# Moving six of sixteen row tiles of p @ w_ple away from attention, into the router's gap and in front of the tail

## The chip, the cores and the metric

The kernel runs on one core of one Trainium2 chip. A core has five engines that run side by side and wait for each other by semaphores: PE (TensorE, matrix products into the banks of PSUM), DVE (VectorE), ACT (ScalarE), POOL (GpSimd) and SP (SyncE, which here issues most DMAs). Each engine works through its own row of instructions in order. The metric is the time of one execution on the device, in microseconds (us).

## The reference

One encoder layer over x (2048 rows of 1024, f32). What follows is the order of the work, cut to what matters here:

```python
h = rms_norm(x, g_mix);  q, k, v, u = split(h @ w_in)
ya = attention_group(q, k, v)        # 8 query heads, 2 key heads of 64, all 2048 keys
yh = hyena_group(u)                  # two gated long convolutions by FFT, 512 channels
x = x + concat(group_rms(ya), group_rms(yh)) @ w_out
x = x + hierarchical_moe(rms_norm(x, g_moe))      # 32 experts, two per row
gate = sigmoid(rms_norm(x, g_ple) @ w_ple_gate + b_ple_gate)
x = x + (p @ w_ple) * gate           # p: 2048 x 256, w_ple: 256 x 1024
return rms_norm(x, g_final)
```

The change is about `p @ w_ple`. It depends on nothing but inputs, so it can be computed at any time before the last gate; sixteen tiles of 128 rows make up the 2048 rows.

## The kernel before, in words

`block_kernel` writes the work of two sides in turn. The left side is the input projection and then `Attention.run`; the right side is the filters of hyena, hyena itself, and what follows it. `interleave` (L91) always takes the next piece from the side that has come less far, by costs that the pieces yield, scaled with `SHARE`. An engine runs its instructions in the order in which they come out of this, so the order is fixed when the program is built.

Attention works in units of one head and half of the queries (16 units). A unit has 16 steps over key tiles: score products L798 and L801 into a PSUM bank, exp on ACT (L802), and the products with v (L811). Between them stand the products L733 and maxima L735 that prepare later units. At a unit's end L833 sums the rows, SP carries the sums through DRAM, and L850 on DVE scales the output. Scores use two banks (pool `at_ps`); a third comes from the pool `at_px`, which is opened some units after the right side has said `K.banks_free = True`:

```python
wait -= K.banks_free
if wait == -BANKS_AFTER:
    psx = self.pool("at_px", 1, space=PSUM)
```

The pool is opened `BANKS_AFTER` = 2 units after the flag. Its bank lies where banks of the right side lay, and so the first product that uses it waits for the last user of these.

Hyena has three kinds of steps here. A pair is a transform back of one tile (L539 on PE, its gate L541 on DVE, named z) followed by the next transform (L499). A middle step (`mid`) loads zt and ab, multiplies by w (L294, tile ph<-zt), multiplies by the filter on DVE (L523, tile ab), goes back (L307, tile ph<-ab), and is copied by ACT (L527) and stored. The last transforms back are L539 and L541 alone. All of them share one PSUM tile of two banks, ph.

p @ w_ple is computed in two ways. `Ple` splits p and w_ple into a high and a low fp32r part: per tile two transposes L1514, and for each of two column halves six products L1529 to L1531, a copy to the SBUF tile ob by ACT (L1532; two buffers), and when both halves are there a store to DRAM, pp_d, by SP (L1534). `LatePle` uses plain f32, L1570, and keeps its result in SBUF. Before the change tiles 0 to 3 are late (`PLE_LATE`), 4 to 6 run on the right side behind hyena (`PLE_N`), after a delay that counts as progress (`PLE_LAG`), and 7 to 15 run behind `stage_out`, while the router works out which row goes to which expert: that stretch is called the router's gap. The router's small products there are L1131, L1157, L1158, L1169 and L1170; its tile ep holds the number of blocks of each expert. SP reads these numbers one by one into registers (L1359, 31 TENSOR_LOADs), and also issues the store and the load of a small table (L1221, tile ov_eb; L1223, tile ebr).

The experts start with casts of the raw weights on ACT (L1301), products L1322 to L1324 and, for rows beyond full blocks, f32 products L1328. The tail loads rows x and the experts' results, normalises them (xn, DVE L1635), transposes them (L1642), multiplies by w_ple_gate (L1652 to L1654) and combines the gate with the product pp. Its tile t takes pp from SBUF where it is late, else it loads it from pp_d (`Tail.tiles`, L1611). `LatePle.run` stands just ahead of it in PE's row.

## Time and profile before

| | us |
|---|---|
| median of three runs | 3171.41 (3170.64 to 3173.77) |
| the profiled execution | 3178.87 |
| its span | 3177.1 |
| PE busy | 2905.4 (91%) |
| DVE busy | 2047.3 (64%) |
| ACT busy | 1322.0 (42%) |
| POOL busy | 1143.2 (36%) |

The profiled execution is one of its own, 7.46 us longer than the median of the runs, and 1.8 us of it lie outside the span. In the timeline's rows an idle time in brackets stands behind an instruction that its engine had to wait for, with what released it last. Products on PE overlap, so one that is shown with 0.40 us may start 0.23 us behind the one ahead of it. PEclk in the windows is the granted clock as a share of 2.4 GHz.

### The profile page before, as it was taken

The numbers are of one execution on the slowest core, as the hardware profiler recorded it, in microseconds if no ns is written. First come the engines' busy times: TensorE is split into PE (matmuls) and PEld (weight loads), VectorE is DVE, ScalarE is ACT, GpSimd is POOL, SyncE is SP. The second block draws the span as 40 slices with busy tenths as digits, with TensorE's granted clock in tenths as the row PEclk, the third lists the DMA queues.
The fourth block names the chain that finished last, engine by engine and source line by source line (L and its number), as shares of the span: only waits on it lengthen the run. The fifth ranks groups of instructions, "written<-read, shape, count | busy, mean of one in ns | idle before, by whom it ended". The sixth has DMA issues, their size and how long they took to land. (4 is left out here: it accounts for less than half of the span.)

```text
span 3177.1 us, 50424 instructions
## 1 busy us (share of the span) xinstructions
PE 2905.4 (91%) x19001; PEld 1937.3 (61%) x19001; DVE 2047.3 (64%) x2737; ACT 1322.0 (42%) x1975; POOL 1143.2 (36%) x1058
## 2 busy tenths in 40 slices
PE   7989889798899999759999999989999999998897
PEld 5757667575445453524444488856667777675776
DVE  5865656536677776628887745366667677675665
ACT  3232233332344434225444422245556566664332
POOL 1423323242355555218877643011111211121443
PEclk9989889898999999879999999989999999999999
DMA  6477787786755765651000254379789888897553
GB/s 196 146 219 245 212 251 238 225 262 187 222 164 171 204 179 168 177 170 44 18 12 15 65 168 140 137 230 337 249 274 340 292 305 284 309 322 250 180 180 112
DMA packets 471989, 627.45 MB, mean 197 GB/s; under 512 B 64597, under 2 KB 302984, under 8 KB 467262
## 3 DMA queue, kind: packets, MB, share of 16 engines
q1 hardware_dynamic: 451630, 568.73, 55.7%
q0 software_dynamic: 20112, 55.47, 5.5%
q8 instruction: 150, 2.46, 0.3%
q14 instruction: 97, 0.79, 0.1%
HBM read 462.45 MB, written 161.56 MB: 196 GB/s over the span
## 5 line engine op out<-in xcount | busy, mean ns | idle before, releaser
L1306 DVE TENSOR_TENSOR wl<-raw,wh 128x1024 fp32r<-128x1024 f32 x384 | 462.8, 1223 | 202.2 <-ACT wh L1301 192.8
L1301 ACT CAST wh<-raw 128x1024 fp32r<-128x1024 f32 x384 | 398.2, 1051 | 262.9 <-PE ps L1324 87.5
L821 POOL TENSOR_TENSOR sums<-e,sums 128x512 f32<-128x512 f32 x306 | 412.4, 1364 | 145.9 <-ACT e L802 135.7
L802 ACT ACTIVATE e<-ps 128x512 f32<-128x512 f32 x512 | 290.1, 596 | 330.8 <-PE ps L801 278.5
L735 DVE TENSOR_REDUCE mx<-pa 128x1 f32<-128x512 f32 x512 | 330.1, 683 | 100.9 <-PE pa L733 100.2
L811 PE MATMUL po<-e,v 128*64 128x512 f32 x1024 | 290.0, 624 | 0.0
L1401 POOL DMA_DIRECT2D y_d<-ob x64 | 36.0, 564 | 556.8 <-DVE ob L1400 349.4
L1322 PE MATMUL ps<-wh,xt 128*128 128x512 f32 (+4 forms) x512 | 212.8, 416 | 9.5 <-ACT wh L1301 9.3
L1323 PE MATMUL ps<-wl,xt 128*128 128x512 f32 (+4 forms) x512 | 207.5, 405 | 7.1 <-DVE wl L1306 7.1
L1324 PE MATMUL ps<-wh,xt 128*128 128x512 f32 (+4 forms) x512 | 203.6, 398 | 0.0
L148 PE MATMUL ps<-xh,wh 128*128 128x512 f32 x384 | 157.7, 411 | 8.1 <-ACT U L204 8.1
L733 PE MATMUL pa<-kst,q 128*128 128x512 f32 x352 | 140.3, 450 | 22.6 <-DVE mx L735 20.2
L149 PE MATMUL ps<-xl,wh 128*128 128x512 f32 x384 | 159.3, 415 | 0.0
L150 PE MATMUL ps<-xh,wl 128*128 128x512 f32 x384 | 158.0, 411 | 0.4 <-POOL wl L88 0.4
L88 POOL TENSOR_TENSOR wl<-raw,wh 128x2048 fp32r<-128x2048 f32 (+1 forms) x26 | 102.8, 3956 | 150.3 <-ACT wh L138 144.8
L798 PE MATMUL ps<-q,kst 128*128 128x512 f32 x352 | 151.5, 431 | 3.6 <-ACT e L802 3.6
L801 PE MATMUL ps<-q,k 65*128 65x512 f32 x352 | 141.9, 403 | 4.7 <-DMA q<-mr 4.7
L821 DVE TENSOR_TENSOR sums<-e,sums 128x512 f32<-128x512 f32 x110 | 120.5, 1102 | 34.7 <-ACT e L802 34.0
L733 PEld LDWEIGHTS pa<-kst,q 128*128 128x128 f32 x352 | 63.3, 191 | 123.1 <-DVE mx L735 73.0
L1271 POOL DMA_INDIRECT g<-h_d,idx x52 | 74.5, 1433 | 165.5 <-PE pt L1289 66.4
L148 PE MATMUL ps<-wh,xh 128*128 128x256 f32 x384 | 121.6, 317 | 4.7 <-ACT xh L79 2.4
L1322 PEld LDWEIGHTS ps<-wh,xt 128*128 128x128 f32 (+4 forms) x512 | 96.0, 188 | 47.0 <-ACT wh L1301 13.7
(370 smaller groups left out, 6631.5 us busy)
## 6 DMA issues: line engine op xcount, KB each, us to landing
raw<-in_w_gate_dram SPq DMA_DIRECT2D x128, 512.0 KB
raw<-in_w_up_dram SPq DMA_DIRECT2D x128, 512.0 KB
raw<-in_w_down_dram SPq DMA_DIRECT2D x128, 512.0 KB
h_f<-hs SPq DMA_DIRECT2D x256, 128.0 KB
ab<-h_f SPq DMA_DIRECT2D x32, 1024.0 KB
raw<-in_w_in_dram SPq DMA_DIRECT2D x30, 1024.0 KB
xt<-in_x_dram SPq DMA_DIRECT2D x32, 512.0 KB
dec<-in_c_decay_dram SPq DMA_DIRECT2D x64, 256.0 KB
```

Of the source, the lines that this page charges most:

```text
L148: nc.tensor.matmul(ps, lh, rh, start=(k == 0), stop=False)
L149: nc.tensor.matmul(ps, lh, rl, start=False, stop=False)
L733: nc.tensor.matmul(pa, qh[:, t * P:(t + 1) * P], self.kst[g][:, q * 512:(q + 1) * 512], start=True, stop=True)
L735: nc.vector.tensor_reduce(out=mx[:, t, q:q + 1], in_=pa, axis=AX.X, op=ALU.max)
L802: nc.scalar.activation(out=pe[:, i], in_=ps, func=AF.Exp, scale=0.125)
L811: mm = nc.tensor.matmul(po[H2[i]], v[:, kt, g * 64:(g + 1) * 64], pe[:, i], start=(kt == 0), stop=(kt == NT - 1), skip_group_check=True)
L821: acc[j][1].tensor_tensor(out=sums[j], in0=pe[:, i], in1=src, op=ALU.add)
L1301: nc.scalar.copy(hi, raw)
L1306: nc.vector.tensor_tensor(out=lo, in0=raw, in1=hi.bitcast(F32), op=ALU.subtract)
L1322: nc.tensor.matmul(ps[:m], xt[:, k, 0, :m], hv[:, j], start=(k == 0), stop=False)
L1323: nc.tensor.matmul(ps[:m], xt[:, k, 0, :m], lv[:, j], start=False, stop=False)
L1324: nc.tensor.matmul(ps[:m], xt[:, k, 1, :m], hv[:, j], start=False, stop=(k == 7))
```

## The change

The three tiles of the right side are taken away, together with their delay, their own loading of the weights and their numbers (`PLE_N`, `PLE_LAG`, the fourth share). The router's gap takes tiles 6 to 15, ten instead of nine, and tiles 0 to 5 are late, six instead of four. `LatePle` transposes its rows in two groups of four and two tiles, the pool for pp in the tail has six buffers instead of four, and `Tail.tiles` loads x for the tiles 4 and 5 itself, without a load of pp.

```diff
@@ -42,11 +42,9 @@
 SUM_POOL = [2] * 16
 PV_LAG = 2
 BANKS_AFTER = 2
-PLE_N = 3
 ROUTE_AT = 0
-PLE_LATE = 4
-PLE_LAG = 5.0
-SHARE = (0.56, 1.0, 0.8, 1.6)
+PLE_LATE = 6
+SHARE = (0.56, 1.0, 0.8)
 
 
 def rows_bcast(ap, parts=P):
@@ -1551,10 +1549,12 @@
             pr = px.tile([P, PLE_LATE, 256], F32, name="pr")
             nc.sync.dma_start(pr, p_in[:PLE_LATE * P].rearrange("(t p) n -> p t n", p=P))
             for k in range(2):
-                pt = pst.tile([P, 512], F32, tag="pt", name="pt")
-                for t in range(PLE_LATE):
-                    nc.tensor.transpose(pt[:, t * P:(t + 1) * P], pr[:, t, k * P:(k + 1) * P], K.ident)
-                nc.scalar.copy(self.pT[:, k].rearrange("p t c -> p (t c)"), pt[:, :PLE_LATE * P])
+                for t0 in range(0, PLE_LATE, 4):
+                    pt = pst.tile([P, 512], F32, tag="pt", name="pt")
+                    n = min(4, PLE_LATE - t0)
+                    for t in range(n):
+                        nc.tensor.transpose(pt[:, t * P:(t + 1) * P], pr[:, t0 + t, k * P:(k + 1) * P], K.ident)
+                    nc.scalar.copy(self.pT[:, k, t0:t0 + n].rearrange("p t c -> p (t c)"), pt[:, :n * P])
 
     def run(self, pool):
 
@@ -1582,7 +1582,7 @@
         self.K, self.x1_d, self.pp_d = K, x1_d, pp_d
         pool = lambda name, bufs, **k: st.enter_context(tc.tile_pool(name=name, bufs=bufs, **k))
         pc, self.pl, praw = [pool(f"ta_{n}", b, side=K.side) for n, b in (("c", 1), ("l", 4), ("raw", 2))]
-        pw, self.pp = pool("ta_w", 2, side=K.side), pool("ta_p", 4)
+        pw, self.pp = pool("ta_w", 2, side=K.side), pool("ta_p", PLE_LATE)
         self.bc = {}
 
         with tc.issue_after(after):
@@ -1604,9 +1604,9 @@
         return x2
 
     def tiles(self, t):
-        if t < len(self.done):
-            return self.loaded.pop(0), self.done[t]
-        x2 = self.load(t)
+        x2 = self.loaded.pop(0) if self.loaded else self.load(t)
+        if t < PLE_LATE:
+            return x2, self.done[t]
         pp = self.pp.tile([P, D], F32, tag="pp", name="pp")
         self.K.nc.sync.dma_start(pp, self.pp_d[t * P:(t + 1) * P])
         return x2, pp
@@ -1826,12 +1826,6 @@
                     yield c * SHARE[2]
             s_hc.close()
             yield None
-            yield PLE_LAG * SHARE[3]
-            with ExitStack() as s1:
-                ple.open(s1, K.side)
-                ple.weights()
-                for c in ple.run(s1, range(PLE_LATE, PLE_LATE + PLE_N)):
-                    yield c * SHARE[3]
             K.banks_free = True
             pw = s_w.enter_context(tc.tile_pool(name="ou_w", bufs=2, side=K.side))
             with tc.tile_pool(name="ou_r", bufs=2, side=K.side) as praw:
@@ -1848,7 +1842,7 @@
                           A["b_group"], A["w_router"][0], A["b_router"], x1_d, h_d, lg, R, ple.weights)
             s_w.close()
             with ExitStack() as s2:
-                for n, _ in enumerate(ple.run(s2, range(PLE_LATE + PLE_N, NT), 3, K.side)):
+                for n, _ in enumerate(ple.run(s2, range(PLE_LATE, NT), 3, K.side)):
                     if n == ROUTE_AT:
                         R.finish(A["c_caps"])
             late = LatePle(K, st, A["p"][0, 0], A["w_ple"][0])
```

Line numbers of the kernel after are two lower than those before, up to the `Ple` class; L1570 and what follows it have the same numbers in both.

On PE, at the unit end that lies at 1236.28 us in the trace (sums are row sums, kst and k keys, bt and z tiles of hyena), the kernel before goes on like this:

```order
L833 MATMUL pa<-sums,sel 32x512 x3
L733 MATMUL pa<-kst_6073,qh 128x512 x2
L539 MATMUL ph<-bt,wb 64x512 x2
L798 MATMUL ps<-q_11301,kst_6073 128x512
L801 MATMUL ps<-q_11301,k_6074 128x512
L798 MATMUL ps<-q_11301,kst_6073 128x512
L801 MATMUL ps<-q_11301,k_6074 128x512
L833 MATMUL pa<-osq,sel 32x512
L733 MATMUL pa<-kst_6073,qh 128x512 x2
L499 MATMUL ph<-z,w1d 128x512 x2
L798 MATMUL ps<-q_11301,kst_6073 128x512
L801 MATMUL ps<-q_11301,k_6074 128x512
```

The kernel after, at the same unit end and then at the end of hyena's work:

```order
L831 MATMUL pa<-sums,sel 32x512 x3
L731 MATMUL pa<-kst_6073,qh 128x512 x2
L537 MATMUL ph<-bt,wb 64x512 x2
L831 MATMUL pa<-osq,sel 32x512
L731 MATMUL pa<-kst_6073,qh 128x512 x3
L497 MATMUL ph<-z,w1d 128x512 x2
L731 MATMUL pa<-kst_6073,qh 128x512 x4
L537 MATMUL ph<-bt,wb 64x512 x2
...
L305 MATMUL ph<-ab,wa 64x128 x32
L537 MATMUL ph<-bt,wb 64x512 x16
L796 MATMUL ps<-q_11344,kst_6073 128x512
L799 MATMUL ps<-q_11344,k_6074 128x512
```

Before, score products (L798, L801) stand between hyena's pairs; after, the first of them (L796, L799) stands behind the last of hyena's L537, with four pairs and eight middle steps ahead of it.

On PE in the router's gap (rt_ tiles are the router's, pr and ph, plh, pll are PLE's), before:

```order
L1131 MATMUL rt_ps<-rt_i_15551,rt_oh_15544 32x193
L1157 MATMUL rt_ps<-rt_f_17623,rt_i_15554 128x32
L1158 MATMUL rt_ps<-rt_f_17623,rt_i_15554 64x32
L1514 MATMUL pt<-ident,pr 128x128 x2
L1529 MATMUL pp<-plh,ph 128x512
L1530 MATMUL pp<-pll,ph 128x512
L1531 MATMUL pp<-plh,pl 128x512
L1529 MATMUL pp<-plh,ph 128x512
L1530 MATMUL pp<-pll,ph 128x512
L1531 MATMUL pp<-plh,pl 128x512
L1169 MATMUL rt_ps<-ident,rt_f_17638 128x32 x2
```

And after:

```order
L1129 MATMUL rt_ps<-rt_i_15448,rt_oh_15441 32x193
L1512 MATMUL pt<-ident,pr 128x128 x2
L1527 MATMUL pp<-plh,ph 128x512
L1528 MATMUL pp<-pll,ph 128x512
...
L1529 MATMUL pp<-plh,pl 128x512
L1155 MATMUL rt_ps<-rt_f_17520,rt_i_15451 128x32
L1156 MATMUL rt_ps<-rt_f_17520,rt_i_15451 64x32
L1527 MATMUL pp<-plh,ph 128x512
...
L1529 MATMUL pp<-plh,pl 128x512
L1167 MATMUL rt_ps<-ident,rt_f_17535 128x32 x2
```

The transposes of a tile and one column half have moved ahead of the router's first small products, and another half stands ahead of the next ones.

On SP, behind the register loads of ep and around the load of the table ebr, before:

```order
L1534 DMA pp_d<-ob 128x1024
L1223 DMA ebr<-ov_eb 1x128
L1359 TENSOR_LOAD ep
L1359 ISA x2
L1534 DMA pp_d<-ob 128x1024
L1359 TENSOR_LOAD ep
```

And after:

```order
L1532 DMA pp_d<-ob 128x1024
L1221 DMA ebr<-ov_eb 1x128
L1357 TENSOR_LOAD ep
L1357 ISA x2
L1357 TENSOR_LOAD ep
L1357 ISA x2
L1532 DMA pp_d<-ob 128x1024
L1357 TENSOR_LOAD ep
L1357 ISA x2
L1357 TENSOR_LOAD ep
L1357 ISA x2
...
L1357 ISA x2
L1532 DMA pp_d<-ob 128x1024
```

Before, the last store of pp_d stood one register load behind ebr. After, two stores stand behind it, the second behind six register loads.

## Rows read from the trace of the kernel before

**Rows 1.** Windows: stretch and length, busy us and (instructions) of each engine, granted clock, DMA share, GB/s.
```profile
core 0: us, PE busy (x) PEld busy (x) DVE busy (x) ACT busy (x) POOL busy (x), PEclk, DMA share, GB/s
1302.00:1390.00 88.00, 48.94 (x594) 29.21 (x593) 29.82 (x43) 6.66 (x7) 1.64 (x1) 0.65 0.63 177
1508.00:1736.00 228.00, 226.01 (x884) 105.85 (x887) 182.06 (x265) 103.74 (x188) 177.99 (x133) 1.00 0.07 17
2140.00:2400.00 260.00, 260.00 (x1382) 177.09 (x1380) 175.59 (x179) 150.91 (x183) 37.97 (x50) 1.00 0.82 288
```

**Rows 2.** Timeline of PE, ends of units: start, duration, line, out<-in.
```profile
1236.28 1.06 PE L833 MATMUL pa<-sums,sel 128*32 128x512 f32 x6
...
1468.76 0.63 PE L833 MATMUL pa<-sums,sel 128*32 128x512 f32 x3
...
1507.91 0.63 PE L833 MATMUL pa<-sums,sel 128*32 128x512 f32 x3
...
1735.72 1.06 PE L833 MATMUL pa<-sums,sel 128*32 128x512 f32 x6
```

**Rows 3.** Timeline of PE, hyena's middle steps and transforms back.
```profile
1273.25 0.99 PE L294 MATMUL ph<-zt,w 64*64 64x128 f32 x28
...
1302.56 1.98 PE L307 MATMUL ph<-ab,wa 64*64 64x128 f32 x64 [0.49 <-PE pa L833]
...
1328.60 1.30 PE L294 MATMUL ph<-zt,w 64*64 64x128 f32 x32
...
1340.86 3.69 PE L307 MATMUL ph<-ab,wa 64*64 64x128 f32 x64 [2.52 <-issue]
1345.71 1.98 PE L294 MATMUL ph<-zt,w 64*64 64x128 f32 x32 [1.17 <-ACT sg L527]
...
1354.67 1.08 PE L539 MATMUL ph<-bt,wb 128*64 128x512 f32 x4 [1.17 <-ACT sg L527]
...
1387.76 1.98 PE L539 MATMUL ph<-bt,wb 128*64 128x512 f32 x4 [1.85 <-DMA bt<-t_z]
```

**Rows 4.** Timeline of PE, PLE's first transpose and attention's resumption.
```profile
1399.25 0.66 PE L1514 MATMUL pt<-ident,pr 128*128 128x128 f32 x2 [9.52 <-DMA pr<-in_p_dram]
...
1416.45 0.50 PE L733 MATMUL pa<-kst,q 128*128 128x512 f32 x1 [0.67 <-ACT ob L1532]
```

**Rows 5.** Timeline of DVE, the scaling at a unit's end.
```profile
1259.44 1.31 DVE L850 SCALAR_TENSOR_TENSOR ob<-ob,gcol 128x512 f32<-128x512 f32 x1 [3.19 <-DMA ob<-r_d]
```

**Rows 6.** Timeline of PE in the router's gap.
```profile
2079.46 0.41 PE L1157 MATMUL rt_ps<-rt_f,rt_i 32*128 32x32 f32 x2 [1.47 <-DVE rt_f L1067]
...
2080.88 0.69 PE L1514 MATMUL pt<-ident,pr 128*128 128x128 f32 x2 [0.79 <-DMA pr<-in_p_dram]
...
2084.11 1.06 PE L1169 MATMUL rt_ps<-ident,rt_f 32*128 32x32 f32 x4
```

**Rows 7.** Timeline of ACT: a copy of PLE, the experts' first cast.
```profile
2080.61 1.07 ACT L1532 COPY ob<-pp 128x512 f32<-128x512 f32 x2 [7.18 <-DMA pp_d<-ob]
...
2112.54 1.99 ACT L1301 CAST wh<-raw 128x1024 fp32r<-128x1024 f32 x2 [10.80 <-DMA pp_d<-ob]
```

**Rows 8.** Timeline of SP's DMA queue at the end of the gap.
```profile
2106.08 0.27 SPq L1223 DMA_DIRECT2D ebr<-ov_eb  x1
2107.24 0.33 SPq L1534 DMA_DIRECT2D pp_d<-ob  x1
2114.97 2.85 SPq L1298 DMA_DIRECT2D raw<-in_w_gate_dram  x3
```

**Rows 9.** Timeline of PE at the start of the tail.
```profile
2919.07 14.00 PE L1570 MATMUL ps<-lpw,lpT 128*128 128x512 f32 x32 [1.03 <-ACTq L1416]
2945.80 1.97 PE L1642 MATMUL pt<-ident,xn 128*128 128x128 f32 x8 [12.73 <-DVE xn L1635]
2950.73 0.79 PE L1652 MATMUL ps<-wgh,th 128*128 128x512 f32 x1 [2.96 <-ACT th L79]
...
2954.09 0.40 PE L1652 MATMUL ps<-wgh,th 128*128 128x512 f32 x1
```

**Rows 10.** Timeline of DVE, the tail's second normalised tile.
```profile
2951.97 1.28 DVE L1635 SCALAR_TENSOR_TENSOR xn<-x,ss,gp 128x1024 f32<-128x1024 f32 x1
```

## The prediction

> **What bounds the kernel now.** I read the busy time of TensorE (PE) stage by stage first [rows 1]; the reader is to see where PE is full, because there removed work is time and delayed work is time too. PE is full in attention's later part (226.01 of 228 us) and in the experts (260.00 of 260). Between them lie stretches where it isn't, and the change touches three. In the first, 1302 to 1390, PE has 48.94 us of work in 88 and a granted clock of 0.65, a mean between the two levels, 1.2 and 2.4 GHz: attention is at a standstill there and hyena runs alone. Its scores have got a second PSUM pool, and its bank lies where the right side's banks lay, so the first score product that takes it stands in PE's row until the right side is through. The second is the router's gap, where PE and the first expert wait for small transfers. The third is the start of the tail, where PE waits for the first normalised tile.
>
> The timeline of PE at the ends of attention's units (the sums of one head and half, L833) gives the pace [rows 2]: one unit ends at 1236.28, another runs beside hyena until the standstill, and the one behind the standstill ends at 1468.76. From 1507.91 to 1735.72 lie five units, (1735.72 − 1507.91)/5 = 45.56 us each: that is attention with nothing beside it.
>
> In the standstill two kinds of work follow each other [rows 3]. The middle steps of hyena (L294, an add on DVE, L307, a copy on ACT) are serial: from 1328.60 to 1354.67 three of them take 26.07, 8.69 us each. The inverse transforms back run from 1354.67 to their last product at 1387.76, and with its 2 us and the product on DVE behind it to about 1390.7, 36 us; then comes PLE, the product p @ w_ple [rows 4]: PE's first transpose at 1399.25 after 9.52 us for the load of p, and attention goes on at 1416.45.
>
> **The change part by part.** *Beside attention.* It removes three tiles (36 products), the loads and casts of the weights, and a delay that counted as progress of the right side. In time that is 1416.45 − 1390.7 = 25.8 us of the standstill. But the order also shows that attention gets its extra bank one unit earlier: at the boundary of 1236.28 the scores now stop, and the rest of hyena, four pairs of L539/L499, eight middle steps and the last sixteen L539, comes before the next score. So the unit that ran from there on beside hyena runs later, alone.
>
> The sum: hyena alone from 1236.28. Its four pairs can't end before the rope row on DVE, L850, which starts at 1259.44 since it waits for a transfer [rows 5], and the last z stands behind it on DVE and the load of the next stage behind that on SP; beside attention the first L294 came at 1273.25 [rows 3]. I take 1266, the middle of 1260 and 1273.25. Eight middle steps at 8.69 are 69.5, the way back is 36: attention resumes at 1266 + 69.5 + 36 = 1371.5, 45.0 earlier than now. Then one unit more has to be done alone, +45.6; the unit that follows the resumption took 1468.76 − 1416.45 = 52.3 and stays as it is. Together **+0.6**. Ends: the start at 1260 gives −5; the start at 1273.25 with middle steps of 9.37 gives 1273.25 + 75.0 + 36 = 1384.2, +13.4. The 9.37 is 8.69 plus 0.68, the difference between L294 as it is at 1328.60 and at half clock, 1.30 against 1.98 [rows 3]; L307 is at half clock in those steps already (3.69, against 1.98 at 1302.56).
>
> Here a rule speaks against the change: the standstill gets longer (from 1302–1416 to some 135 us), with PE about half idle. The rows say that the clock falls in it: 0.65 [rows 1], and L539 takes 1.98 at its end where it took 1.08 at 1354.67 [rows 3]. The Trainium skill, "TensorE: Matmul & The Clock Gate", section "HAM oscillation — how this bites in real kernels", says that bursts of products between waits can find PE at half rate every time, so that the waits cost twice. The trace agrees for this stretch; by the rule the sum would go to its upper end, which is the second rival below.
>
> *In the router's gap.* Ten tiles instead of nine. The tenth tile's own work on PE, two half tiles, is hidden: a half tile takes 2.5 us at half clock, between the transpose and L1169 (2081.57 to 2084.11) [rows 6], so at most 5, and the first expert's products wait for weights until 2112.54. What isn't hidden lies on two queues. First, PE's row: a transpose and half a tile (six products) now stand ahead of L1157, and another half ahead of L1169. In the trace that transpose waited for p until 2080.88, and its half tile couldn't start earlier either, since ACT's copy at 2080.61, after 7.18 us idle, frees its bank [rows 6, 7]. So the router's L1157 moves from 2079.46 to about 2084.0, and L1169, behind L1157's 0.3 and the second half tile's 2.5, from 2084.11 to 2086.8: +2.7 for what follows from it, the counts (ep), the table of the overflow and its way back (ebr). Second, SP: the first cast of the experts, L1301 on ACT at 2112.54, waits 10.80 us for the landing of the last pp_d store, issued at 2107.24; landing takes 5.3 us [rows 7, 8]. That store stands on SP behind ebr (2106.08). Between them SP now has more: two register loads of ep, the store of tile 14, four more loads, the store of tile 15. With ten such loads between that store and the next DMA at 2114.97, 0.74 us each, the last store comes 6 × 0.74 + 2 × 0.33 = 5.1 us behind ebr instead of 1.16: +3.9. Together +6.6 for the first cast. Of the f32 work L1328 that follows, some is done while it waits, −0.6. **+6.0**; PE is full from there on, so that the shift stays. Ends: 0, when the order of PE costs nothing (p's load early, ebr no later) and the last store lands under another wait; +12, when the copy ob has to wait for a buffer as it does here for 7.18 us [rows 7] and the whole chain follows.
>
> *In front of the tail.* Six tiles instead of four: 4 tiles took 14.00 us, two more are 7.0, and behind them PE is idle for 12.73 us until the first transpose at 2945.80 [rows 9], which waits for DVE. They fit, with 5.7 to spare. In the new order the last tile's products and the second tile's transposes come before the first gate product. The second xn on DVE starts at 2951.97 and takes 1.28 [rows 10], while the first gate product now starts at 2950.73: if it has to wait for 2953.3 and the transposes, it loses up to 3.6. Against it, PE comes from a shorter pause: transposes in 1.97 and the eight gate products from 2950.73 to 2954.09 in 3.36 are at half clock, and full clock would give back half of each, 1.0 + 1.7 = 2.7. Two loads of pp and two places on SP go. I take **−0.5**, ends −3 and +4.
>
> *Else.* The transposes for six tiles need two PSUM tiles instead of one, in the gap behind PLE, four transposes and two copies more: under 2 us, before the wait for the first cast, so hidden by it; if that cover went, +2, within the +12. Of SBUF nothing that waits changes.
>
> Sum: +0.6 + 6.0 − 0.5 = **+6.1**. On the profiled execution, 3178.87 (1.8 us of it outside its span), that is 3185.0. The median of the runs is 7.46 lower, 3171.41; the difference is carried over: **3177.5**.
>
> **Rivals.**
> 1. *The gap costs nothing* (no change). The first cast moves by 0 to 2 us: if p's load for the next tile has landed when it is wanted and ebr is ruled by something else than PE's row. For it: ebr is released by a transfer. Against it: the order of SP, six loads ahead of the last store. Then +0.6 + 1 − 0.5 = +1.1: 3172.5.
> 2. *Half clock through the whole standstill* (more slowly). Middle steps at 9.37 and the late start: +13.4 + 6 − 0.5 = +18.9: 3190. For it: L294 at 1.98 at 1345.71 [rows 3]. Against it: 1.30 at 1328.60, in the same run of steps.
> 3. *Full clock in the middle steps* (faster). Hyena alone starts straight from a stretch in which attention fills PE; if PE keeps the upper level, a step loses 3.69 − 1.98 = 1.71, and eight of them 13.7: resume at 1357.8, −13.1 for attention, and with +6.0 − 0.5 it is −7.6: 3164. The sum falls below zero from four such steps on (6.1/1.71 = 3.6). For it: L307 at 1302.56, just behind attention, took 1.98. Against it: 3.69 at 1340.86, with the same pauses [rows 3]. A lesser gap cost would lead to the same place from smaller gains.
> 4. *The bank doesn't stop the scores a unit earlier*, since the pool's place in PSUM isn't where hyena's banks are: then attention goes on beside hyena, the 25.8 us of PLE fall away: −25.8 + 6 − 0.5 = −20: 3151. Against it: the order itself, in which no score stands before the last L539.
>
> **How the numbers follow.** The forecast has 0.42, rival 1 0.23, rival 2 0.15, rival 3 0.15, rival 4 0.05. A measurement of this kernel tells 0.2%, 6.3 us, from no change. The forecast's own range is 3171 to 3186, and it lies on the border: of its 0.42, 0.26 is slower and 0.16 within 6.3. Rival 1 is within (0.17) with 0.03 slower and 0.03 faster, rival 2 slower, rival 3 faster but for 0.04, rival 4 faster. Slower 0.26 + 0.03 + 0.15 = 0.44; same 0.16 + 0.17 + 0.04 = 0.37; faster 0.03 + 0.11 + 0.05 = 0.19. The range, 3162 to 3192, takes in rivals 1 to 3 and leaves rival 4 and the farther parts of 2 and 3 out.
>
> **What would show it.** In the profile of the changed kernel: scores that stop at about 1237 and resume at 1365 to 1384, with no L1529 in between; L307 in 3.69 there (right) or in 1.98 (rival 3); units of 45 us to the end of attention; the first L1301 cast of the experts, measured from the end of the last attention unit, 6 us later than now, behind a pp_d store that stands six loads after ebr; 48 products L1570 in one stretch of 21 us and less than 6 us idle before the first tail transpose. The forecast is wrong if the resumption is outside 1365 to 1384, or if the first cast doesn't move.

## The result and the profile after

The changed kernel takes 3187.35 us (median of 12 runs, 3175.86 to 3193.05), the kernel before 3168.1 (12 runs, 3154.2 to 3176.8). The ratio is 1.006, with a 95% interval from 1.0047 to 1.0073: 15 to 23 us slower. The forecast was slower by 6.1, in a range that holds the measured time; the direction was right and the size about a third.

The profiled execution of after has a span of 3189.7 us, 12.6 more than the span before. That is less than the timed difference, and the unit ends show why: up to the one that [rows 2] show at 1236.28 both kernels have the same instructions in the same order, and after reaches it at 1224.63. In eleven other profiles of kernels with the same instructions up to there it lies at 1220.0 to 1230.2, so the one profile of before had been slow by some 10 us there. Stretches are therefore compared from here on, each from an event to another inside one execution, and over several kernels that share the stretch:

| stretch | as before | as after | difference | forecast |
|---|---|---|---|---|
| sixth unit end to attention's last unit end | 581.5, 581.5, 578.8, 580.8 | 590.1, 589.5, 585.4, 586.4, 583.7 | +6.4 | +0.6 |
| last unit end to the gap's first product L1529 | 236.1, 234.5, 237.9, 238.2 | 239.1, 239.3, 236.7, 240.7, 240.6 | +2.6 | 0 |
| that product to the experts' first L1322 | 59.8, 61.9, 64.1, 63.2 | 66.8, 66.1, 67.7, 65.4 | +4.3 | +6.0 |
| first late product to the last gate product | 239.7, 243.4, 243.4, 240.4 | 250.0, 248.5, 245.2, 247.5, 248.3, 247.7 | +6.1 | −0.5 |

Each list begins with one of the two kernels of the change; the other numbers are those of experiments below that have the stretch in the same form. The differences are those of the means. The sum is +19.4, and the timing says +19; the two stretches left out, the experts up to the first late product and what follows the last gate product, differ by under 0.5. Experiments 2 and 4 are left out of the third row: there ten tiles stand beside the set-up of four late ones (66.3), or nine beside the set-up of six (65.5), so that they have the form of neither kernel.

**The standstill.** Two windows of after from the sixth unit end (columns as in [rows 1]), with the first 8.8 us of the second by themselves:

```profile
1224.60:1354.20 129.60, 71.06 (x861) 40.36 (x860) 40.37 (x53) 13.37 (x14) 1.64 (x1) 0.67 0.68 199
1354.20:1417.70 63.50, 56.32 (x182) 24.65 (x183) 41.67 (x41) 31.30 (x52) 41.73 (x28) 0.88 0.25 75
1354.20:1363.00 8.80, 8.80 (x20) 5.28 (x20) 1.97 (x3) 4.20 (x7) 3.76 (x3) 0.50 0.48 149
```

And PE's timeline in the same stretch (L292 and L305 are the middle steps, L537 the last transforms back, L796 a score product):

```profile
1224.63 1.06 PE L831 MATMUL pa<-sums,sel 128*32 128x512 f32 x6
...
1251.87 1.98 PE L292 MATMUL ph<-zt,w 64*64 64x128 f32 x32 [3.91 <-DMA zt<-s_z]
1256.41 3.69 PE L305 MATMUL ph<-ab,wa 64*64 64x128 f32 x64 [2.56 <-DVE ab L521]
...
1272.95 1.98 PE L305 MATMUL ph<-ab,wa 64*64 64x128 f32 x64 [2.52 <-issue]
...
1318.45 1.97 PE L537 MATMUL ph<-bt,wb 128*64 128x512 f32 x4 [1.17 <-ACT sg L525]
...
1351.44 1.98 PE L537 MATMUL ph<-bt,wb 128*64 128x512 f32 x4 [2.86 <-DMA bt<-t_z]
1354.19 0.80 PE L796 MATMUL ps<-q,kst 128*128 128x512 f32 x1 [0.78 <-DVE z L539]
...
1397.83 0.80 PE L731 MATMUL pa<-kst,q 128*128 128x512 f32 x1 [3.85 <-DVE q L726]
...
1417.68 0.63 PE L831 MATMUL pa<-sums,sel 128*32 128x512 f32 x3
```

Scores stop at the sixth unit end, as the order said, and hyena runs alone: 27 us to the first middle step, eight steps of (1318.45 − 1251.87)/8 = 8.3 us, 36 for the way back. The scores come back at half clock (0.80 and 0.63 us instead of 0.50 and 0.40), 0.50 granted for 8.8 us, and the unit takes 63.5 us against the 52.3 of before [rows 2, 4].

**The gap.** ACT, then SP, then PE in after (L1530 copies to ob, L1299 is the experts' first cast, L1532 the store of pp_d, L1221 ebr, L1155 and L1167 the router's products), which answer to [rows 6 to 8]:

```profile
2100.36 0.59 ACT L1530 COPY ob<-pp 128x512 f32<-128x512 f32 x1 [0.99 <-PE pp L1529]
2110.61 1.07 ACT L1530 COPY ob<-pp 128x512 f32<-128x512 f32 x2 [9.65 <-DMA pp_d<-ob]
...
2117.23 5.79 ACT L1299 CAST wh<-raw 128x1024 fp32r<-128x1024 f32 x6 [4.57 <-DMA pp_d<-ob]
```

```profile
2104.52 0.27 SPq L1221 DMA_DIRECT2D ebr<-ov_eb  x1
2106.25 5.78 SPq L1532 DMA_DIRECT2D pp_d<-ob  x2
```

```profile
2081.37 0.63 PE L1155 MATMUL rt_ps<-rt_f,rt_i 32*128 32x32 f32 x2
...
2085.13 1.06 PE L1167 MATMUL rt_ps<-ident,rt_f 32*128 32x32 f32 x4
```

The first cast comes 4.7 us later than before; from attention's last unit end it is 7.8, of which 3.1 lie ahead of the gap. PE's row isn't why: L1155 moved by 1.9 us and L1167 by 1.0, and ebr is issued 1.6 us earlier than before. The tenth tile's copy stood on ACT for 9.65 us until one of the two buffers ob was free, that is until an earlier store had landed; then its own store had to land.

**The tail.** PE in after (x is the number of records; 20 + 16 + 4 + 8 of L1570 are six tiles):

```profile
2923.39 8.85 PE L1570 MATMUL ps<-lpw,lpT 128*128 128x512 f32 x20 [1.03 <-ACTq L1414]
2935.56 8.83 PE L1570 MATMUL ps<-lpw,lpT 128*128 128x512 f32 x16 [3.32 <-ACT pp L1571]
2946.40 3.28 PE L1570 MATMUL ps<-lpw,lpT 128*128 128x512 f32 x4 [2.01 <-ACT pp L1571]
2949.47 1.47 PE L1642 MATMUL pt<-ident,xn 128*128 128x128 f32 x8
2950.78 3.60 PE L1570 MATMUL ps<-lpw,lpT 128*128 128x512 f32 x8
2956.94 1.79 PE L1642 MATMUL pt<-ident,xn 128*128 128x128 f32 x8 [2.56 <-DVE xn L1635]
2958.42 0.79 PE L1652 MATMUL ps<-wgh,th 128*128 128x512 f32 x1
```

The idle time of 12.73 us [rows 9] is used up, and the 48 late products don't come in one stretch of 21 us: PE waits 3.32 and 2.01 us for ACT's copies of them, so that they last from 2923.39 to 2954.38, 31 us. Between the first tile's transposes and the first gate product now stand the last late products and a wait for the second xn: 2958.42 − 2949.47 = 9.0 us, against 4.9 before.

### The profile page after: what moved, and what is told of

Its sections match the earlier page's. It is cut to its first block, busy times and chain, and to the rows that moved or that the text cites. A ratio compares the mean times of both kernels' runs of the same rounds, so it can differ in the third digit from the quotient of the medians.

```text
span 3189.7 us, 50374 instructions
## 1 busy us (share of the span) xinstructions
PE 2917.1 (91%) x18993; PEld 1941.9 (61%) x18993; DVE 2045.9 (64%) x2733; ACT 1321.6 (41%) x1973; POOL 1137.2 (36%) x1058
## 4 chain that ended last, share of the span: by engine, by line
PE 59%; DMA 15%; DVE 8%; issue 4%; POOL 2%; ACT 2%; SPq 1%; DVEq 0%; POOLq 0%; ACTq 0%
PE po L809 6%; PE ps L1320 4%; PE ps L1321 4%; PE ps L1322 4%; PE pa L731 3%; PE ps L796 3%; PE pr L1326 3%; PE ps L799 3%; DMA zt<-s_f 2%; PE ps L1386 2%; PE ps L1388 2%; PE ps L146 2%; PE ps L1387 2%; PE ph L305 2%; PE ps L147 2%
## 5 line engine op out<-in xcount | busy, mean ns | idle before, releaser
L1299 ACT CAST wh<-raw 128x1024 fp32r<-128x1024 f32 x384 | 399.0, 1053 | 262.2 <-PE ps L1322 80.7
L819 POOL TENSOR_TENSOR sums<-e,sums 128x512 f32<-128x512 f32 x306 | 412.5, 1365 | 127.9 <-ACT e L800 122.1
L1322 PE MATMUL ps<-wh,xt 128*128 128x512 f32 (+4 forms) x512 | 203.4, 397 | 0.0
L796 PE MATMUL ps<-q,kst 128*128 128x512 f32 x352 | 152.4, 433 | 5.7 <-ACT e L800 4.8
L731 PE MATMUL pa<-kst,q 128*128 128x512 f32 x352 | 139.2, 446 | 17.8 <-DVE mx L733 12.6
L799 PE MATMUL ps<-q,k 65*128 65x512 f32 x352 | 143.0, 406 | 4.1 <-DMA q<-mr 4.1
L1326 PE MATMUL pr<-raw,xr 128*32 128x128 f32 (+1 forms) x2112 | 125.7, 303 | 1.7 <-issue 1.3
```

The source lines that it names most:

```text
L731: nc.tensor.matmul(pa, qh[:, t * P:(t + 1) * P], self.kst[g][:, q * 512:(q + 1) * 512], start=True, stop=True)
L796: mm = nc.tensor.matmul(ps, self.kst[g][:, ks], qh[:, ql_s[i]], start=True, stop=False)
L819: acc[j][1].tensor_tensor(out=sums[j], in0=pe[:, i], in1=src, op=ALU.add)
L1299: nc.scalar.copy(hi, raw)
L1322: nc.tensor.matmul(ps[:m], xt[:, k, 1, :m], hv[:, j], start=False, stop=(k == 7))
```

## The experiments

Differences are to the kernel before, from the ratio's interval times 3168. The edits are cut to the lines that matter; what stands behind a # is not in the code.

**1. The first part alone** (`a_only`): no tiles beside attention, the rest as before.

```diff
-            yield PLE_LAG * SHARE[3]
-            with ExitStack() as s1:
-                ple.open(s1, K.side)
-                ...
+        u = t + 3 if t < 7 else t          # Tail.tiles
+        self.K.nc.sync.dma_start(pp, self.pp_d[u * P:(u + 1) * P])
```

> The first part alone: no tile of p @ w_ple beside attention, gap (nine tiles) and tail (four late tiles) as before. Tiles 4 to 6 are left out; the tail reads the products of tiles 7 to 9 in their place. Theory 1 (the standstill moves a unit earlier and its end is cold): +6 to +10 us against the kernel before, nearly all of it between the unit end at about 1230 us and the last unit end; the first unit after the standstill takes 60 us or more instead of 52, with its first products at half clock, since no products of p @ w_ple run ahead of it any more. Rival (the difference of the two profiles in this stretch is scatter from execution to execution, as the 11.7 us are by which the same instructions ended earlier at the unit end before it): -3 to +3 us, and a first unit of 52 to 55 us.

Measured: 3184.74, +8 to +19 us. The stretch of attention took 589.5 us, and the first unit behind the standstill 59.1, just short of the 60 named and well above the rival's 52 to 55. That unit, in windows of this kernel and of the one with ten tiles in the gap, which has the tiles beside attention:

```profile
1360.50:1419.60 59.10, 54.37 (x181) 24.16 (x181) 37.94 (x41) 31.27 (x52) 44.88 (x28) 0.89 0.26 81
```

```profile
1404.90:1458.10 53.20, 48.30 (x179) 20.64 (x178) 39.95 (x41) 30.11 (x51) 44.97 (x28) 1.00 0.26 80
```

The same 180 products keep PE busy for 54.4 us at a clock of 0.89 and for 48.3 at 1.00; the idle time is the same, 4.7 and 4.9. The products of p @ w_ple had brought PE to full clock before attention came back, as PE's timeline in the second kernel shows, from PLE's first product to attention's first score:

```profile
1387.73 0.79 PE L1529 MATMUL pp<-plh,ph 128*128 128x512 f32 x1 [0.46 <-ACT ph L79]
...
1393.53 0.39 PE L1530 MATMUL pp<-pll,ph 128*128 128x512 f32 x1
...
1404.87 0.39 PE L798 MATMUL ps<-qh,kst 128*128 128x512 f32 x1
```

The loss is in the stretch itself and not scatter.

**2. The second part alone** (`b_only`): tile 6 computed in the gap too.

```diff
-                for n, _ in enumerate(ple.run(s2, range(PLE_LATE + PLE_N, NT), 3, K.side)):
+                for n, _ in enumerate(ple.run(s2, range(PLE_LATE + PLE_N - 1, NT), 3, K.side)):
```

> The second part alone: ten tiles in the router's gap instead of nine, by computing tile 6 there a second time; beside attention and tail as before. On PE the row ahead of L1157 is as before, on SP the last store of pp_d stands five register loads behind the table load ebr instead of one. Theory 1 (the last store's place on SP sets the experts' start): +3 to +5 us, the first cast of the experts behind the landing of the last store, 4 us later. Rival A (PE's row ahead of L1157 is what counts, and it isn't changed here): 0 to +1 us. Rival B (a buffer of ob is waited for once more): +7 us or more.

Measured: 3176.42, +1 to +12. The first product of the experts came 66.3 us behind the gap's first, as in after, though PE's row ahead of L1157 is that of before. So that part of the order costs no more than the scatter. The last copy waited 9.13 us for a buffer here too: that is rival B's mechanism, at some 4 us (66.3 against a mean of 62.3) instead of 7 or more.

**3. A wider lpT alone** (`place_only`). In the profile of after the first cast of the tail's weights waits 7 us for a y_d store, since lpT is 2 KB wider and what lies behind it has moved. I took this for the tail's loss.

```diff
-        self.pT = pc.tile([P, 2, PLE_LATE, P], F32, name="lpT")
+        self.pT = pc.tile([P, 2, 6, P], F32, name="lpT")[:, :, :PLE_LATE]
```

> No work is moved at all: the SBUF tile lpT, which holds the transposed rows of the late tiles, is made as wide as six tiles need (2 KB more on each partition), while four are used as before. What lies behind it in SBUF moves by 2 KB. Theory 1 (the tail's cost is one of place: the first cast of the tail's weights now lies where the experts' results are stored from, waits for the last y_d store, and holds ACT's row): +6 to +9 us, the first cast of wgh at ten us or more after the overflow stage's end instead of 3. Rival (the tail's cost comes from the order of PE's row, in which the second tile's transposes and the last late product stand ahead of the first gate product): 0 us.

Measured: 3167.54, −6 to +3 us: nothing. The wait is there, on ACT, and PE's first transposes and first gate product come all the same:

```profile
2912.99 1.99 ACT L79 CAST wgh<-wgr 128x1024 fp32r<-128x1024 f32 x2 [6.21 <-DMA y_d<-ob]
```

```profile
2928.32 1.97 PE L1642 MATMUL pt<-ident,xn 128*128 128x128 f32 x8 [7.38 <-DVE xn L1635]
2930.11 0.79 PE L1652 MATMUL ps<-wgh,th 128*128 128x512 f32 x1
```

The late products begin at 2904.13, so the first gate product is 26.0 us behind them, 5.7 sooner than before. My theory of the tail fell. Every kernel below with six late tiles has the wider lpT as well, so this kernel, and not the one before, is the right one to compare them with in the tail.

**4. The third part alone** (`c_only`): six late tiles, the other two stages as before.

```diff
+PLE_N = 3                       # on the changed kernel; PLE_LAG and SHARE as before
+                for c in ple.run(s1, range(4, 7)):          # beside attention again
-                for n, _ in enumerate(ple.run(s2, range(PLE_LATE, NT), 3, K.side)):
+                for n, _ in enumerate(ple.run(s2, range(7, NT), 3, K.side)):
```

> The third part alone: six late tiles in front of the tail, by computing tiles 4 and 5 there again; beside attention (tiles 4 to 6) and gap (7 to 15) as before. Theory 1 (place): as with the wider lpT alone, +6 to +9 us, and no more than 2 us beyond it for the two tiles' work and PE's order. Rival (PE's order): +6 to +9 us here, where the wider lpT alone costs nothing. If the tail's difference was scatter: -2 to +2 us.

Measured: 3182.27, +7 to +18 us. The first gate product is 34.7 us behind the first late one (35.0 in after, 30.4 to 31.7 with four late tiles, 26.0 with four and the wider lpT), and the last gate product 248.5. The rival's case: PE's row. In the gap, with nine tiles, the last copy of p @ w_ple waits for a buffer here too:

```profile
2100.54 1.07 ACT L1532 COPY ob<-pp 128x512 f32<-128x512 f32 x2 [10.01 <-DMA pp_d<-ob]
```

The three parts alone add up to +32, with about 10 either way; the change as a whole to +19. The difference of 13 is barely beyond the noise; part of c_only's time (9 us more than the others between the experts' start and the tail) is unexplained.

**5. Extra products at the end of the standstill** (`warm`).

```diff
+        for i in range(WARM if o else 0):          # WARM = 8, in back(o, b, q)
+            nc.tensor.matmul(bk[H2[i % 2], 1], K.wb, fl(bt[:, (i % 2) * 4:(i % 2) * 4 + 4]), ...)
```

> The changed kernel, with eight extra products on PE behind each of hyena's last transforms back, into the unused half of ph (their result is not read): work that does nothing but keep PE busy at the end of the standstill, as the products of p @ w_ple did before. Theory 1 (the first unit behind the standstill is slow because PE comes to it at half clock): that unit has a granted clock near 1.00 instead of 0.88 and takes 52 to 55 us instead of 59 to 63.5; the whole is +13 us against the kernel before instead of the change's +19. Rival (the unit is slow because DVE's row is held by the casts of w_out, in which the q of the next unit stands): it still takes 58 us or more, and the whole stays at +17 to +22.

Measured: 3227.65, +46 to +65. The edit was badly aimed: it put the extra products into all transforms back of the second order, of which many run beside attention. Only the end of the standstill can be read:

```profile
1383.34 1.08 PE L539 MATMUL ph<-bt,wb 128*64 128x512 f32 x4 [0.80 <-DVE z L543]
1388.65 0.49 PE L800 MATMUL ps<-q,kst 128*128 128x512 f32 x1 [0.79 <-DVE z L543]
...
1434.11 0.80 PE L735 MATMUL pa<-kst,q 128*128 128x512 f32 x1 [6.58 <-DVE mx L737]
```

The scores start at full clock (0.49), but the unit takes 62.6 us at a granted clock of 0.89, since PE then waits 6.58 us for DVE and is at half clock again (0.80). Inconclusive: the rival's number came, with a share of both causes.

**6. The bank two units later** (`banks4`).

```diff
-BANKS_AFTER = 2
+BANKS_AFTER = 4
```

> The changed kernel with BANKS_AFTER = 4: attention gets its extra PSUM bank two units later. In PE's order the scores then go on beside hyena's pairs and middle steps for two more units and stop only for the last transforms back. Theory 1 (the wait for that bank makes the standstill, and its place decides its length): a standstill of about 36 us instead of 131, two units of about 61 us beside hyena, and from the unit end at 1225 to the last one some 515 to 535 us instead of 590; the whole 35 to 60 us faster than the kernel before. Rival (hyena's steps would stop attention anyway, by DVE, ACT or the transfers, and two units on two banks cost what is saved): 570 us or more in that stretch, the whole within 10 us of the kernel before.

Measured: 3142.1, ratio 0.9906 (0.9883 to 0.9929), 22 to 37 us faster than before. Windows from the seventh unit end to the eighth, and to the ninth:

```profile
1289.00:1360.00 71.00, 66.40 (x715) 36.81 (x715) 51.94 (x70) 25.65 (x44) 35.11 (x27) 0.95 0.45 129
1360.00:1458.00 98.00, 76.69 (x260) 30.01 (x250) 62.12 (x73) 33.83 (x56) 47.27 (x29) 0.84 0.48 132
```

The standstill is 43 us, and the whole stretch 539.7 instead of 587. The unit beside hyena's middle steps took 71.5, not 61, so that the gain falls short of the 35 to 60 named, and the stretch lies just above 515 to 535; the rival's 570, and its 10 us, are far off. The wait for the bank makes the standstill.

**7. The late tiles in two lots** (`late_split`).

```diff
-            for t in range(PLE_LATE):
+            return [self.one(pool, psm, "lp", t) for t in range(FIRST)]          # FIRST = 4
-            return x2, self.done[t]
+            return x2, self.done[t] if t < FIRST else self.late.one(self.pp, self.psm, "pg", t)
```

> The changed kernel, with the late tiles in two lots: four in front of the tail, as before the change, and the fifth and sixth among the tail's first tiles. The first gate product then has the first tile's transposes alone ahead of it in PE's row. Theory 1 (the tail's loss is PE's order ahead of the first gate product): from the first late product to the first gate product 31 us or less instead of 35, to the last gate product 240 to 245 instead of 250; the whole +11 to +15 us against the kernel before. Rival (the loss is the two tiles' work itself, 7 us wherever it stands, since PE is full in the tail): the first gate product is earlier, but the last one isn't, 248 us or more, the whole +17 to +21.

Measured: 3183.14, +9 to +19 us; by time alone it can't be told from the change. In its profile the gate follows the first transposes at once:

```profile
2945.34 1.97 PE L1644 MATMUL pt<-ident,xn 128*128 128x128 f32 x8 [7.08 <-DVE xn L1637]
2947.13 0.79 PE L1654 MATMUL ps<-wgh,th 128*128 128x512 f32 x1
```

26.1 us behind the first late product, 9 sooner than in after, and the last gate product at 244.4 instead of 245 to 250: theory 1's numbers, and not the rival's 248. So about half of what was lost up to the last gate product came back; the rest the two tiles take inside the tail, where PE has 9 to 15 us of idle time in all. A longer stretch shows more: from the experts' first product to the end of the span the three kernels with two lots (this one and the two of 11 and 12) take 1059.9 to 1063.1 us, as the four with four late tiles do (1060.2 to 1065.4), against 1066.6 to 1072.6 with six in one lot, without c_only. Part of that lies ahead of the tail (800 us to the first late product instead of 803 to 807), for a reason that isn't shown.

**8. The stores of pp_d from ACT** (`store_act`).

```diff
-            nc.sync.dma_start(self.pp_d[t * P:(t + 1) * P], ob)
+            nc.scalar.dma_start(self.pp_d[t * P:(t + 1) * P], ob)
```

> The changed kernel, with the stores of pp_d in the router's gap issued by ACT instead of SP, so that none stands behind SP's register loads of ep. Theory 1 (the last store's place in SP's row holds back the experts' first cast): that cast comes 58 to 60 us behind the gap's first product of p @ w_ple, as with nine tiles, instead of 62 to 63; the whole +14 to +17 us against the kernel before. Rival (PE's row ahead of L1157 and the tenth tile's own chain of copies set it): 62 us or more, the whole +18 to +21.

Measured: 3194.63, +15 to +29. ACT in the gap (ACTq is its DMA queue):

```profile
2095.70 0.33 ACTq L1532 DMA_DIRECT2D pp_d<-ob  x1
...
2107.56 1.07 ACT L1530 COPY ob<-pp 128x512 f32<-128x512 f32 x2 [9.31 <-DMA pp_d<-ob]
...
2108.66 0.33 ACTq L1532 DMA_DIRECT2D pp_d<-ob  x1
...
2111.53 6.73 ACT L1299 CAST wh<-raw 128x1024 fp32r<-128x1024 f32 x7 [1.91 <-DMA pp_d<-ob]
```

The store whose buffer the tenth tile's copy takes is issued at 2095.70, behind nothing of SP's, and the copy still starts at 2107.56. SP's row, on which 3.9 of the predicted 6.0 us rested, isn't the cause.

**9. Four buffers ob** (`ob4`).

```diff
+        pob = st.enter_context(tc.tile_pool(name="pl_ob", bufs=OB, side=side))          # OB = 4
-            ob = px.tile([P, D], F32, tag="ob", name="ob")
+            ob = pob.tile([P, D], F32, tag="ob", name="ob")
```

> The changed kernel, with four buffers for the copies ob in the router's gap instead of two. Theory 1 (the gap's loss is the tenth tile's wait for a buffer: its copy on ACT stands 9 to 10 us until an earlier store of pp_d has landed, and then its own store has to land before the experts' first cast): no copy in the gap waits more than 2 us for a store, and the first cast comes 57 to 60 us behind the gap's first product of p @ w_ple instead of 62 to 63; the whole +12 to +16 us against the kernel before. Rival (what holds the first cast is the landing of the last store, which is slow beside the experts' first weights however early it is issued): the copies don't wait, the cast stays at 61 us or later, the whole +18 to +21.

Measured: 3190.82, +14 to +27. No copy waits for a store, and the first cast comes 47.7 us behind the gap's first product, 15 earlier, at 2094.81; but the first expert product comes 68.3 us behind the gap's first. PE, and SP:

```profile
2095.01 7.13 PE L1327 MATMUL pr<-raw,xr 128*64 128x256 f32 x64
2109.56 1.09 PE L1559 MATMUL pt<-ident,pr 128*128 128x128 f32 x4 [7.42 <-issue]
...
2115.42 0.79 PE L1321 MATMUL ps<-wh,xt 128*128 128x512 f32 x1 [0.46 <-ACT lpT L1560]
```

```profile
2084.64 14.18 SPq L1535 DMA_DIRECT2D pp_d<-ob  x4
...
2102.14 0.38 SPq L1548 DMA_DIRECT2D lpw<-in_w_ple_dram  x1
```

The four buffers moved the set-up of `LatePle` (its loads, and twelve transposes L1559) behind the last stores, and PE's row waits for that instead. Neither theory had this: one wait was taken away and another took its place.

**10. The first part with the standstill where it was** (`a_banks3`): experiment 1 with one number changed.

```diff
-BANKS_AFTER = 2
+BANKS_AFTER = 3
```

> The first part alone (no tile beside attention; tiles 4 to 6 left out, their products read from tiles 7 to 9; gap and tail as before), with BANKS_AFTER = 3, so that the scores stop at the same unit end as in the kernel before. Theory 1 (the loss of the first part is made of one unit more behind the standstill and a cold first unit, both against some 49 us won): the standstill is about 90 us instead of 116, the first unit behind it takes 58 to 60 us instead of 53, from the unit end at about 1230 to the last one 558 to 565 us instead of 581; the whole 14 to 22 us faster than before. Rival A (the first unit isn't slower for want of the warm-up): 53 us, 552 to 557, the whole 23 to 30 faster. Rival B (taking the tiles away costs for another reason than the place of the standstill): the whole within 6 us of before or slower.

Measured: 3147.42, ratio 0.9933 (0.991 to 0.9956): 14 to 29 us faster than before. The end of the standstill and the unit behind it:

```profile
1377.23 1.98 PE L539 MATMUL ph<-bt,wb 128*64 128x512 f32 x4 [1.96 <-DMA bt<-t_z]
1379.99 0.80 PE L733 MATMUL pa<-kst,q 128*128 128x512 f32 x1 [0.78 <-DVE z L541]
```

```profile
1380.60:1437.00 56.40, 51.63 (x179) 22.37 (x177) 37.67 (x41) 30.86 (x51) 44.41 (x28) 0.92 0.29 89
```

The standstill is 87.9 us and the stretch 557.1, 24 less than before. The unit takes 56.4, 3 more than with the tiles ahead of it, which lies between theory 1 (58 to 60) and rival A (53). So taking the tiles away is worth what it looks like, as long as the standstill stays at its place; the same edit with `BANKS_AFTER` = 2 lost 13 us.

**11 and 12. Three edits together** (`best_4`, `best_5`): the changed kernel with `BANKS_AFTER` 4 or 5, the late tiles in two lots, four buffers ob.

```diff
-BANKS_AFTER = 2
+BANKS_AFTER = 5
+OB = 4
+FIRST = 4
```

> The changed kernel with three edits together: BANKS_AFTER = 4, the late tiles in two lots, and four buffers ob in the gap. Theory 1 (the three terms add): the 28 us that BANKS_AFTER = 4 alone was faster than the kernel before, 5 for the late lots and 3 for the buffers, 36 us faster, 31 to 42. Rival (the tail and the gap take back what is given): 25 to 30 faster.

> As the kernel with three edits, but BANKS_AFTER = 5: in PE's order the last transforms back stand between scores too, and nothing of hyena runs alone. Theory 1: no standstill of more than 5 us; of the 43 us in which PE waited there some 10 to 15 come back as work beside the scores, so 25 to 30 us faster than with BANKS_AFTER = 4, 60 to 68 faster than the kernel before. Rival (a unit on two score banks and beside the last transforms, which wait for loads, is slower by as much): within 6 us of BANKS_AFTER = 4.

Measured: 3137.8 with 4, ratio 0.9898 (0.9877 to 0.992), and 3107.2 with 5, ratio 0.9803 (0.9779 to 0.9828): 25 to 39 and 55 to 70 us faster than the kernel before. The first lies between theory 1's 36 and the rival's 25 to 30 and settles neither; in the second theory 1's time came. Windows of the latter, the eighth and the ninth unit:

```profile
1287.00:1358.00 71.00, 66.64 (x731) 37.18 (x726) 52.51 (x71) 25.73 (x44) 35.20 (x27) 0.95 0.46 131
1358.00:1425.00 67.00, 62.92 (x260) 27.05 (x254) 48.56 (x69) 31.73 (x54) 40.05 (x28) 1.00 0.64 178
```

Nothing of hyena runs alone any more, and the ninth unit has the full clock to its end; the stretch is 511.3 us. The longest stop of the scores there is 8.3 us, not 5. The gap gave nothing back in either: 68.9 and 70.2 us from its first product to the experts' first, more than the 65.4 to 67.7 of the table. What the tail gave is in experiment 7.

## Why the prediction was right, and where it was wrong

The direction and the range hold, but +6.1 became +19, and that the range took this in is in part luck. It reached so far up for hyena's middle steps at half clock (rival 2); what was lost came instead from the first unit behind the standstill, which the sum had unchanged, and from the tail, whose +6.1 lies beyond the end of +4 that was named.

*The standstill moves a unit earlier.* Right, and shown by experiment 10 against experiment 1: they differ in one number, and their ratios to before are 0.9933 and 1.0042, some 35 us apart. The resumption, 129.6 us behind the sixth unit end, would be at 1365.8 on the clock of [rows 2], just inside the 1365 to 1384 outside which the forecast was to be wrong. The pieces of the sum were +0.6 = −45.0 + 45.6. Measured over the kernels of the table: from the sixth unit end the scores come back after 178.7 us before and after 129.7 now, −49.0, since the four pairs took less than assumed and a middle step 8.3 us instead of 8.69; the rest behind the first unit is longer by 49.0, not 45.6. The step that failed is "the unit that follows the resumption ... stays as it is": it took 53.0 us before and 58 to 63.5 now, +6.4 by the mean of 59.4. The two score pairs that had gone ahead of the standstill make up under 1 of that; the clock the most: PE's busy time in this unit is 5.4 us longer, its idle time 1.1, by the means. The prediction had seen that the clock falls in the standstill and had priced it there, in hyena's products, where it cost less than allowed. It had counted the 36 products that went as standstill saved and as nothing else, and they were what brought PE back to full clock. That removing them costs this is shown by experiments 1 and 2; putting other work in their place (experiment 5) did not win it back, so the cure stays unproven. The Trainium skill, "TensorE: Matmul & The Clock Gate", section "HAM oscillation — how this bites in real kernels", says that bursts behind gaps start cold; the trace agrees, with 0.50 granted for the first 8.8 us.

*The router's gap.* Right in sign, with 4.3 instead of 6.0, and for another reason. Both terms of the sum are refuted: PE's row (2.7) by the profile of after and experiment 2, SP's row (3.9) by experiment 8. What stands in their place is the last copy's wait for a buffer, which the prediction had as the mechanism of its upper end: 9.1 to 9.7 us in after and in experiments 2, 7 and 8, and in 5 and 6 shared with a copy ahead of it (7.03 and 4.24, 10.72 and 2.94); with nine tiles and four late ones the last copy waits for no store. But the tenth tile isn't all of its cause: experiment 4, with nine tiles and the set-up of six late ones, has it too (10.01), so the set-up that the prediction called hidden can bring it about as well. That this wait alone makes the 4.3 us isn't shown, since experiment 9 took it away and got another.

*The tail.* Wrong: +6.1 instead of −0.5. Three steps failed. "They fit, with 5.7 to spare" did not hold, since the six tiles' products lasted 31 us and not 21. One more is the offset "full clock would give back half of each, 1.0 + 1.7 = 2.7": the first gate product takes 0.79 us in both, and five of them run at half clock where it had been seven (eight in experiment 4). Another is the wait of the first gate product, "up to 3.6". It seems to have come, 3.8 by the means, from 31.0 to 34.8 us behind the first late product; but that is luck. With the wider lpT and only four tiles in front the gate product comes at 25.9 to 26.5 (experiments 3, 7, 11 and 12), so PE's order costs 8.7 to 9 us, and the wider lpT, for a reason that isn't shown, takes some 5 off. Another 2.3 us were lost from the first gate product to the last, for a cause that stays open. Open is also what six tiles with the narrow lpT would cost: the wait for a y_d store, which cost nothing with four tiles, holds ACT's row ahead of the copies that PE's late products wait for (3.32 and 2.01 us).

*Not forecast*: +2.6 us between attention's last unit and the gap, with a scatter of 4 in either column; in the kernels with `BANKS_AFTER` of 3 to 5 the stretch takes 236.4 to 237.2, as before, so that the missing tiles alone don't make it. Its cause is open.

*The rivals.* No change (the gap costs nothing) fell with the gap's +4.3. Rival 2's time came, +18.9 against +19, without its mechanism: a middle step took 8.3 us, not 9.37, and the start wasn't late. Half clock throughout and full clock in the middle steps both were half true: L305 took 3.58 to 3.69 us in five of the eight steps, 3.27 in one and 1.98 in two. Rival 4 fell with the order.

## What to carry to other kernels

Where a pool's bank is shared between two stages, the place at which it is first asked for decides what runs alone; a count such as `BANKS_AFTER` has to be set again when a part of the stage that frees the bank is taken out. Work that seems to fill an idle place may be what keeps the clock up for what follows, so price the products behind a gap at both levels. And before a long wait is called a cost, take it away, or make it alone: one of 6 us in the tail, made alone, cost nothing, and one of 10 us in the gap gave way to another.

## What was not expected of the hardware

A store of pp_d issued at 2095.70 let go of the copy that takes its buffer at 2107.56, 11.9 us later, and one issued at 2108.66 let go of the next instruction at 2111.53, 2.9 us later (experiment 8), as far as the releasers that the profile names are right: the same store of 128 × 1024, from the same engine, within one stretch. What else the transfers had to do just then was not told apart.
